# Expert stage of a hybrid layer: token rows by indirect DMA and transposes instead of a one-hot gather, second weights in whole rows into four banks, four more weight buffers

## The chip, the cores and the metric

One core of a Trainium2 chip runs the whole layer as one program. The metric is the device time of that program in microseconds: the median of several executions. The kernel before takes 2963.49 us, the median of 3 runs from 2961.25 to 2971.55.

## The reference, cut to what matters

512 tokens of width 2048 go through a layer: attention and RWKV-7 time mixing, an output projection, then a mixture of experts, then a final norm. Everything is float32. Each token goes to 2 of 32 experts (1024 choices in all), and an expert is a gated MLP of width 512:

```python
N_EXPERTS, TOP_K, D_MODEL, D_EXPERT = 32, 2, 2048, 512
h = rms_norm(x, norm_ffn_g) * (1 + sc2) + sh2
expert_idx, gates = hierarchical_route(h, w_grp, b_grp, w_exp, b_exp)
...
xb = x_pad[tok]                                    # rows of the expert's tokens
yb = (silu(xb @ w1[e]) * (xb @ w3[e])) @ w2[e]     # w1, w3: 2048 x 512, w2: 512 x 2048
y  = yb * gate[:, None]
out = zeros.at[slot_tok].add(y)                    # back to the tokens
...
x = x + g2 * out
return rms_norm(x, final_norm_g)
```

The weights of the 32 experts together are 402.65 MB, and all of them are read.

## The kernel before, in words

**Stages.** The program runs the input projection, the attention and the RWKV stage, then the output projection (`out_loop`, L1115), which leaves the residual stream in `xm`: 512 tokens as 4 groups of 128 partitions, 2048 columns each. `route_chunk` (L1267) takes each 512 columns of `xm` as they are finished, transposes them, multiplies them with the router's weights and sums squares for the norm. Then come the choice of experts (L1307 to L1414), the expert stage (L1416 to L1574), and the final norm (L1627 to L1640). A loop over tokens that overflow an expert's slots (L1585) stands behind the expert stage; it runs zero times here.

**Pairs.** Experts are worked in 16 pairs. Each expert has 64 slots, so a pair has 128 rows, and about half of them hold a token. Slot numbers and gates of the tokens are in `sg`; a row with no token is zero.

**Gather.** PE multiplies and adds one-hot matrices to select rows. For this `cut` (L1287) splits `xm` into three bf16 parts `xp0`, `xp1`, `xp2` whose sum is the float32 value; they take 48 KB of each partition. `onehots` (L1422) builds the one-hot matrix `ohb` of a pair on DVE, and by 12 matmuls (L1436) the row `rr` of the slots' norm factors, copied by ACT (L1439). `gather_units` (L1454) is a generator of 16 steps; together they are 192 bf16 matmuls of 128x128 (L1461), which give the tokens' columns already transposed. DVE multiplies with `rr` (L1465) and ACT applies the modulation (L1467) into `xT_`, 16 tiles of 128 columns.

**First layer.** For each quarter q of the 2048 columns, w1 (v = 0) and w3 (v = 1), each with four k and two experts e: a matmul of 64 columns by 512 (L1547), 64 in all. Expert e writes the partitions 64e to 64e + 63 of one PSUM bank, one bank for v = 0 and one for v = 1 (tag "h"). A matmul so uses half of PE's columns, and the two of a (k) use the two halves.

**Middle.** ACT takes the SiLU (L1555, once per pair: the pair's clock mark in the trace), DVE multiplies with the other bank and the gate (L1556), PE transposes (L1559), DVE copies to `gT` (L1561).

**Second layer.** For each 512 of the 2048 output columns n, four j and two experts: 32 matmuls (L1567) into a bank of tag "y" (2 banks). n is the outer loop.

**Scatter.** `scatter_units` (L1471) multiplies `py` with the residual gate (`yt`, L1475), splits it into two float32r parts (ACT cast L168, DVE difference L169), and for each of the 4 token groups multiplies with the one-hot matrix `ohT` (L1480, L1481) into the single bank of tag "o"; DVE adds it to `xm` (L1482). The four units of an n are put on the list `pend`, from which one is taken at each even k of the first layer and after each j of the second. `scatterers` (L1442) makes `ohT` and the gate column.

**Weights.** Each pair has 24 tiles of 1 MB, 16 of w1 and w3 and 8 of w2 (`srcs`). They go through a ring of seven buffers of 16 KB per partition (`fetch` L1210, `wtile` L1224): 2 in `Y` and 1 in `scr`, which are free by then, `NA` = 1 in one pool and `NB` = 3 in another. Nearly all are issued on SP's queue (L1221), each as soon as PE has done with the tile that had the buffer. A tile of w1 or w3 is read in rows of 8 KB; a tile of w2 takes 512 columns of 512 rows, 2 KB each.

**Order.** The program is recorded by the tile framework with a scheduler (`schedule_with_timeline_sim=True`): it simulates the engines and sets the order of each engine's list. The order in which the code emits steps is only its starting point, so gather, scatter and expert matmuls end up interleaved as the simulation had them ready. PE's order is fixed from then on.

PSUM in the expert stage: tags "g" 2 banks (gather), "t" 1, "o" 1, "h" 2, "y" 2.

Of the kernel before, what the change touches and what calls it, by code (L numbers as in the profile page):

```python
# [79 lines left out]
def layer(ctx, tc, tab, x, c, ctx_in, c_ctx, w_mod, b_mod, norm_attn_g, norm_ffn_g, w_in, shift_mu,  # L80
# [29 lines left out]
    r_r = dram.tile([NP0, 128, T], F32, name="r_r")  # L110

# [1080 lines left out]
    NY, NA, NB = 3, 1, 3  # L1192
# [4 lines left out]
    parts = [mq.tile([128, 4, 4, 4, 128], BF16, name=f"xp{i}") for i in range(3)]  # L1197
# [69 lines left out]
    def route_chunk(n):  # L1267
# [16 lines left out]
        if n < 3:  # L1284
            cut(n, ve)

    def cut(n, e):  # L1287
        for i in range(4):
            pa, pb, pc = (p_[:, i, n] for p_ in parts)
            v_ = xm[:, i, 512 * n:512 * n + 512].rearrange("t (p j) -> t j p", j=4)  # L1290
            res = t("res", [128, 4, 128])
            sc.copy(pa, v_)
            e.tensor_sub(res, v_, pa)
            sc.copy(pb, res)
            e.tensor_sub(pc, res, pb)
# [3 lines left out]
    for n in range(3, 4):  # L1299
        cut(n, gp)  # L1300
# [119 lines left out]
    new_psum("ps_moe", [("g", 2, 512), ("t", 1, 512), ("o", 1, 512), ("h", 2, 512), ("y", 2, 512)])  # L1420

    def onehots(pool, psum, base, n):  # L1422
# [10 lines left out]
        prr = psum()[:, 0:n]  # L1433
        for i in range(4):
            for k_ in range(3):
                te.matmul(prr, rb[:, k_, i:i + 1].to_broadcast([128, 128]), ohb[:, i], start=(i + k_ == 0),  # L1436
                          stop=(i + k_ == 5))
# [16 lines left out]
    def gather_units(pool, psum, ohb, rr, xT_, n):  # L1454
        for q in range(4):
            pg = psum()
            for j in range(4):
                first = True
                for part in parts:
                    for i in range(4):  # L1460
                        te.matmul(pg[:, j], part[:, i, q, j], ohb[:, i], start=first, stop=(part is parts[2] and i == 3))  # L1461
                        first = False
                if j == 3:
                    t_ = pool.tile([128, 4, n], F32, name="xr")
                    ve.tensor_mul(t_, pg, rr[:, None, :].to_broadcast([128, 4, n]))  # L1465
                    for jj in range(4):
                        sc.activation(xT_[:, 4 * q + jj], t_[:, jj], AF.Identity, bias=shc[:, q, jj:jj + 1],  # L1467
                                      scale=scc[:, q, jj:jj + 1])
                yield

    def scatter_units(pool, psum, py, ohT, n, np_, done=None):  # L1471
# [5 lines left out]

        def unit(i):
# [33 lines left out]
    for _ in range(4):  # L1512
        next(first)
# [152 lines left out]
```

## Time and profile before

| | before |
|---|---|
| median of 3 runs | 2963.49 us (2961.25 to 2971.55) |
| profiled execution, span | 2957.8 us |
| mean granted PE clock | 0.950 |
| PE busy | 2701.8 us, 91% |
| DVE, ACT, POOL busy | 1634.6, 734.9, 1056.0 us |
| moved by DMA | 715.28 MB, mean 242 GB/s |
| of it on the Pool queue | 75.11 MB |

The span is what the profiler saw from the first instruction to the last; the page gives no further time of that execution, so the span stands beside the median of the unprofiled runs, 5.7 us below it. A row of the profile names the line of the kernel, the engine, the operation and the tiles (out <- in), then counts and times. "PE" is the matmul itself, "PEld" the weight load that overlaps it. 128*64 in a matmul's row is the part of PE's array in use. The expert stage is the last 1.2 ms of the span, from the first SiLU at 1721.9 us on.

### The profile page before, as it was taken

The numbers are of one execution on the slowest core, as the hardware profiler recorded it, in microseconds if no ns is written. First come the engines' busy times: TensorE is split into PE (matmuls) and PEld (weight loads), VectorE is DVE, ScalarE is ACT, GpSimd is POOL, SyncE is SP. The second block draws the span as 40 slices with busy tenths as digits, with TensorE's granted clock in tenths as the row PEclk, the third lists the DMA queues.
The fourth block names the chain that finished last, engine by engine and source line by source line (L and its number), as shares of the span: only waits on it lengthen the run. The fifth ranks groups of instructions, "written<-read, shape, count | busy, mean of one in ns | idle before, by whom it ended". The sixth has DMA issues, their size and how long they took to land. (4 is left out here: it accounts for less than half of the span.)

```text
span 2957.8 us, 45065 instructions
## 1 busy us (share of the span) xinstructions
PE 2701.8 (91%) x18204; PEld 1671.2 (57%) x18204; DVE 1634.6 (55%) x2166; ACT 734.9 (25%) x1366; POOL 1056.0 (36%) x1077
## 2 busy tenths in 40 slices
PE   5999888999977999996888899999999999999995
PEld 3577777887856777884677644333333343333322
DVE  3365788776788777767978523332333332333334
ACT  4222332333333333332234221111111111111102
POOL 1078878067676777777675100000000000000000
PEclk9999898999978899998889899999999999999998
DMA  8955477666678578876563398888888888888996
GB/s 307 326 153 183 133 193 178 140 143 148 145 173 188 163 212 228 231 220 223 174 196 115 146 353 300 297 319 317 318 325 314 304 320 315 318 311 315 334 352 246
DMA packets 563683, 715.28 MB, mean 242 GB/s; under 512 B 319448, under 2 KB 398192, under 8 KB 529424
## 3 DMA queue, kind: packets, MB, share of 16 engines
q1 hardware_dynamic: 454480, 574.78, 59.4%
q0 software_dynamic: 21904, 75.11, 7.8%
q10 hardware_dynamic: 87088, 62.48, 7.2%
q8 instruction: 145, 2.38, 0.3%
q14 instruction: 66, 0.54, 0.1%
HBM read 642.91 MB, written 69.35 MB: 241 GB/s over the span
## 5 line engine op out<-in xcount | busy, mean ns | idle before, releaser
L1482 DVE TENSOR_TENSOR xm<-xm,pox 128x512 f32<-128x512 f32 x256 | 174.9, 687 | 531.3 <-PE pox L1481 531.3
L1636 POOL TENSOR_TENSOR xm<-xm,fgr 128x1024 f32<-128x1024 f32 x2 | 5.6, 2831 | 1271.2 <-ACT xm L1635 1271.2
L523 POOL TENSOR_TENSOR scr<-scr 128x512 f32<-128x512 f32 x240 | 344.7, 1436 | 8.6
L522 POOL TENSOR_TENSOR scr<-scr,scl 128x512 f32<-128x512 f32 x240 | 285.5, 1206 | 145.8 <-DMA scr<-in_w_mod_dram 145.4
L172 PE MATMUL acc<-hT,w 128*128 128x512 f32 (+1 forms) x752 | 269.4, 358 | 8.8 <-DVE km L275 7.4
L174 PE MATMUL acc<-hT,w 128*128 128x512 f32 (+1 forms) x752 | 268.6, 357 | 2.4 <-DVE w L169 2.4
L173 PE MATMUL acc<-hT,w 128*128 128x512 f32 (+1 forms) x752 | 268.4, 357 | 0.0
L1461 PEld LDWEIGHTS <-xp 128*128 128x128 bf16 x3072 | 173.9, 98 | 147.0 <-issue 146.6
L1461 PE MATMUL pg<-ohb,xp 128*128 128x128 bf16 x3072 | 214.3, 220 | 0.0
L1567 PE MATMUL py<-ew,gT 128*64 128x512 f32 x584 | 197.9, 610 | 6.3 <-DVE gT L1561 6.3
L169 DVE TENSOR_TENSOR w<-wraw,w 128x512 fp32r<-128x512 f32 (+1 forms) x132 | 123.3, 939 | 133.2 <-ACT w L168 132.2
L172 PEld LDWEIGHTS acc<-hT,w 128*128 128x128 f32 (+1 forms) x752 | 145.2, 193 | 31.4 <-ACT ks L271 7.5
L174 PEld LDWEIGHTS acc<-hT,w 128*128 128x128 f32 (+1 forms) x752 | 144.4, 192 | 24.6 <-DVE w L169 3.2
L173 PEld LDWEIGHTS acc<-hT,w 128*128 128x128 f32 (+1 forms) x752 | 144.9, 193 | 21.2 <-issue 1.5
L168 ACT CAST yr<-yt 128x512 fp32r<-128x512 f32 x64 | 39.5, 618 | 463.0 <-PE pox L1480 317.4
L518 POOL DMA_DIRECT2D scr<-in_w_mod_dram x128 | 94.5, 738 | 161.0 <-DVE scr L357 141.8
L168 ACT CAST w<-wraw 128x512 fp32r<-128x512 f32 (+1 forms) x132 | 81.0, 616 | 273.7 <-PE acc L173 148.5
L1480 PE MATMUL pox<-yr,ohT 128*128 128x512 f32 x256 | 123.7, 490 | 17.2 <-DVE xm L1482 13.0
L1480 PEld LDWEIGHTS pox<-yr,ohT 128*128 128x128 f32 x256 | 47.7, 187 | 150.7 <-issue 85.7
L1475 DVE TENSOR_TENSOR yt<-py,g2r 128x512 f32<-128x512 f32 x64 | 44.3, 692 | 140.2 <-PE py L1567 140.2
L1567 PE MATMUL py<-Y,gT 128*64 128x512 f32 x288 | 114.1, 616 | 3.1 <-DVE gT L1561 3.1
L478 POOL TENSOR_TENSOR scr<-scr 128x31 f32<-128x31 f32 (+15 forms) x155 | 106.5, 687 | 26.6 <-DMA scr<-r_ab 14.8
(696 smaller groups left out, 5824.1 us busy)
## 6 DMA issues: line engine op xcount, KB each, us to landing
ew<-in_w_dram SPq DMA_DIRECT2D x219, 1024.0 KB, 6.9
Y<-in_w_dram SPq DMA_DIRECT2D x110, 1024.0 KB, 6.8
scr<-in_w_mod_dram POOLq DMA_DIRECT2D x128, 512.0 KB, 5.1
scr<-in_w_dram SPq DMA_DIRECT2D x54, 1024.0 KB, 6.9
ld<-in_w_mod_dram SPq DMA_DIRECT2D x32, 1024.0 KB, 7.0
wraw<-in_w_in_dram ACTq DMA_DIRECT2D x104, 256.0 KB, 3.6
wor<-in_w_out_dram ACTq DMA_DIRECT2D x64, 256.0 KB, 3.5
QXr<-r_qx SPq DMA_DIRECT2D x24, 512.0 KB, 5.3
```

The lines of the kernel that those rows point to most:

```text
L168: sc.copy(hi, src)
L169: (lo_eng or ve).tensor_sub(lo, src, hi)
L172: te.matmul(out, lhs[0], rhs[0], start=first, stop=False)
L173: te.matmul(out, lhs[0], rhs[1], start=False, stop=False)
L174: te.matmul(out, lhs[1], rhs[0], start=False, stop=last)
L478: e.tensor_mul(z, xs.to_broadcast([128, n, m]), ms.to_broadcast([128, n, m]))
L522: gp.tensor_mul(wt[:, k], wt[:, k], s_)
L523: gp.tensor_add(macc, macc, wt[:, k])
L1461: te.matmul(pg[:, j], part[:, i, q, j], ohb[:, i], start=first, stop=(part is parts[2] and i == 3))
L1480: te.matmul(po, ohT[0:np_, 128 * i:128 * i + 128], yr[0], start=True, stop=False)
L1482: ve.tensor_add(xm[:, i, ns], xm[:, i, ns], po)
L1567: te.matmul(py[64 * e:64 * e + 64], gT[:, j, 64 * e:64 * e + 64], ws[e][:, j], start=(j == 0), stop=(j == 3))
```

## The change

- **Rows to DRAM.** `route_chunk` writes each 512 columns of `xm` to a DRAM tile `r_x` by SP's queue. `cut` and the three bf16 parts go.
- **Gather.** `fetch_rows` keeps the one-hot `ohb`, but multiplies it with `tokc`, 6 columns that hold the token number (low and high part) and the three bf16 parts of the norm factor: 4 matmuls of 6 columns. DVE sums them and makes an integer index; an indirect DMA from Pool fetches the rows into `xg` (two buffers, zeroed once), an index of 512 (no token) is out of bounds and fetches nothing; ACT scales the rows by the norm factor. `gather_units` has 4 steps: four float32 transposes into the "t" bank, and four ACT modulations. They are emitted in the first layer's loop at q = 2 and 3, after each v.
- **Second weights.** For pairs 0 to 14 a tile of w2 is 128 whole rows of 8 KB, so the loop over j is outside, n inside, with four open banks of "y". The last pair keeps the old layout and loop.
- **Scatters.** The units of a pair are put on `pend` at its end; `step` takes one at each odd k of the first layer and after each (j, n) of the second.
- **Buffers.** `NA` goes from 1 to 5: eleven weight buffers. PSUM: "t" 1, "o" 1, "h" 2, "y" 4.
- `scatterers` is called after the next pair's `prep`, and the overflow table (`oid`) is worked out behind the first pair's first layer. The overflow loop uses the new helpers.

```diff
+    r_x = dram.tile([T, D], F32, name="r_x")
...
-    NY, NA, NB = 3, 1, 3
+    NY, NA, NB = 3, 5, 3
...
-    parts = [mq.tile([128, 4, 4, 4, 128], BF16, name=f"xp{i}") for i in range(3)]
...
-            srcs += [w2v[2 * p_ + e, :, :, 512 * n:512 * n + 512] for e in range(2)]
+            if p_ < 15:
+                srcs += [w2[0, 2 * p_ + e, 128 * n:128 * n + 128, :] for e in range(2)]
+            else:
+                srcs += [w2v[2 * p_ + e, :, :, 512 * n:512 * n + 512] for e in range(2)]
...
+        sy.dma_start(r_x.rearrange("(i p) d -> p i d", p=128)[:, :, 512 * n:512 * n + 512],
+                     xm[:, :, 512 * n:512 * n + 512])
...
+    tokc = mk.tile([128, 4, 2, 3], BF16, name="tokc")
...
+        gp.tensor_copy(tokc[:, :, 1, k_], left[k_])
...
+    gp.tensor_copy(tokc[:, :, 0, 0], K["pcol"].to_broadcast([128, 4]))
+    gp.tensor_scalar(tokc[:, :, 0, 1], io[:, 0:4], 128.0, -512.0, op0=OP.mult, op1=OP.add)
...
-    new_psum("ps_moe", [("g", 2, 512), ("t", 1, 512), ("o", 1, 512), ("h", 2, 512), ("y", 2, 512)])
...
+    new_psum("ps_moe", [("t", 1, 512), ("o", 1, 512), ("h", 2, 512), ("y", 4, 512)])
+    xgs = [me.tile([128, D], F32, name=f"xg{i}") for i in range(2)]
+    for a_ in xgs:
+        gp.memset(a_, 0.0)
...
-        prr = psum()[:, 0:n]
+        pi = psum()[0:n, 0:6]
         for i in range(4):
-            for k_ in range(3):
-                te.matmul(prr, rb[:, k_, i:i + 1].to_broadcast([128, 128]), ohb[:, i], start=(i + k_ == 0),
-                          stop=(i + k_ == 5))
-        rr = pool.tile([128, n], F32, name="rr", bufs=2)
-        sc.copy(rr, prr)
-        return ohb, rr
+            te.matmul(pi, ohb[:, i], tokc[:, i].rearrange("p a b -> p (a b)"), start=(i == 0), stop=(i == 3))
+        ir = pool.tile([n, 2], F32, name="ir", bufs=2)
+        ve.tensor_reduce(ir, pi.rearrange("p (a b) -> p a b", a=2), axis=AX.X, op=OP.add)
+        ix = pool.tile([n, 1], I32, name="ix", bufs=2)
+        ve.tensor_scalar(ix, ir[:, 0:1], 512.0, None, op0=OP.add)
+        gp.indirect_dma_start(xg, None, r_x, bass.IndirectOffsetOnAxis(ap=ix, axis=0), bounds_check=T - 1,
+                              oob_is_err=False)
+        sc.mul(xg, xg, ir[:, 1:2])
...
-    def gather_units(pool, psum, ohb, rr, xT_, n):
+    def gather_units(psum, xg, xT_, n):
+        v_ = xg.rearrange("s (q p j) -> s q j p", p=128, j=4)
         for q in range(4):
-            pg = psum()
+            pg = psum(q)
             for j in range(4):
-                first = True
-                for part in parts:
-                    for i in range(4):
-                        te.matmul(pg[:, j], part[:, i, q, j], ohb[:, i], start=first, stop=(part is parts[2] and i == 3))
-                        first = False
-                if j == 3:
-                    t_ = pool.tile([128, 4, n], F32, name="xr")
-                    ve.tensor_mul(t_, pg, rr[:, None, :].to_broadcast([128, 4, n]))
-                    for jj in range(4):
-                        sc.activation(xT_[:, 4 * q + jj], t_[:, jj], AF.Identity, bias=shc[:, q, jj:jj + 1],
-                                      scale=scc[:, q, jj:jj + 1])
-                yield
+                te.transpose(pg[:, j], v_[:, q, j], ident[0:n, 0:n])
+            for j in range(4):
+                sc.activation(xT_[:, 4 * q + j], pg[:, j], AF.Identity, bias=shc[:, q, j:j + 1],
+                              scale=scc[:, q, j:j + 1])
+            yield
 
...
+    def step():
+        while pend:
+            if next(pend[0], 0) == 0:
+                pend.pop(0)
+            else:
+                break
...
+        psq = (lambda q: bank("ptg", [128, 4, 128], *(("t", 1), ("o", 1))[q % 2])) if p == 0 else \
+            (lambda q: bank("ptg", [128, 4, 128], "t", 1))
+        return [xT_, gather_units(psq, xg, xT_, 128)]
...
                     if k % 2:
-                        if p < 15:
-                            next(nxt[1], None)
-                    elif pend:
-                        pend.pop(0)()
+                        step()
+                if p < 15 and q > 1:
+                    next(cur_x[1], None)
...
+            pys = [bank("py", [128, 512], "y", 4) for _ in range(4)]
             for j in range(4):
-                for e in range(2):
-                    te.matmul(py[64 * e:64 * e + 64], gT[:, j, 64 * e:64 * e + 64], ws[e][:, j],
-                              start=(j == 0), stop=(j == 3))
-                if pend:
-                    pend.pop(0)()
-            last = p == 15
-            pend += scatter_units(me, psl if last else pso, py, ohT, n, 128, square if last else None)
-            while last and pend:
-                pend.pop(0)()
+                ws = [wtile(w0 + 16 + 2 * j + e) for e in range(2)]
+                for n in range(4):
+                    for e in range(2):
+                        te.matmul(pys[n][64 * e:64 * e + 64], gT[:, j, 64 * e:64 * e + 64], ws[e][:, n],
+                                  start=(j == 0), stop=(j == 3))
+                    step()
+            pend += [scatter_units(me, pso, pys[n], ohT, n, 128) for n in range(4)]
```

**What the scheduler made of it.** PE, second-layer phase of a steady pair before: L1567 alternates between the tiles of the two experts (`scr`, `Y`), all into one bank `py`.

```order
L1567 MATMUL py_17239<-scr_147,gT_17184 64x512
L1567 MATMUL py_17239<-Y_2235,gT_17184 64x512
L1567 MATMUL py_17239<-scr_147,gT_17184 64x512
L1567 MATMUL py_17239<-Y_2235,gT_17184 64x512
L1567 MATMUL py_17239<-scr_147,gT_17184 64x512
```

The same phase after (L1577): four banks, and past the first eight matmuls four of one expert (`ew_16816`), then four of the other (`ew_16818`).

```order
L1577 MATMUL py_16800<-ew_16816,gT_16798 64x512
L1577 MATMUL py_16801<-ew_16816,gT_16798 64x512
L1577 MATMUL py_16802<-ew_16816,gT_16798 64x512
L1577 MATMUL py_16803<-ew_16816,gT_16798 64x512
L1577 MATMUL py_16800<-ew_16818,gT_16798 64x512
L1577 MATMUL py_16801<-ew_16818,gT_16798 64x512
L1577 MATMUL py_16802<-ew_16818,gT_16798 64x512
L1577 MATMUL py_16803<-ew_16818,gT_16798 64x512
```

Before, the halves alternate in the runs of a steady pair; after, two or more of one half follow each other in most of the second layer. Before has one such place, in its first pair's first layer (L1547): `ew_14966` and `ew_14970` are tiles of the first expert, `ew_14968` and `Y` of the second.

```order
L1547 MATMUL ph_15247<-ew_14966,xT__15134 64x512
L1547 MATMUL ph_15247<-ew_14968,xT__15134 64x512
L1547 MATMUL ph_15248<-ew_14970,xT__15134 64x512
L1547 MATMUL ph_15247<-ew_14966,xT__15134 64x512
L1547 MATMUL ph_15247<-ew_14968,xT__15134 64x512
L1547 MATMUL ph_15248<-Y_2235,xT__15134 64x512
L1547 MATMUL ph_15248<-ew_14970,xT__15134 64x512
L1547 MATMUL ph_15248<-Y_2235,xT__15134 64x512
```

Numbering the halves 0 and 1, that is 0 1 0 0 1 1 0 1.

PE, first-layer phase of a steady pair after, where the scatters (L1472, L1473) and the transposes of the next pair's rows (L1458) stand:

```order
L1536 MATMUL ph_16881<-ew_16927,xT__16565 64x512
L1472 MATMUL pox_16961<-yr0_16936,ohT_16570 128x512
L1473 MATMUL pox_16961<-yr1_16937,ohT_16570 128x512
L1472 MATMUL pox_16969<-yr0_16936,ohT_16570 128x512
L1473 MATMUL pox_16969<-yr1_16937,ohT_16570 128x512
L1472 MATMUL pox_16987<-yr0_16982,ohT_16570 128x512
L1473 MATMUL pox_16987<-yr1_16983,ohT_16570 128x512
L1458 MATMUL ptg_16999<-k_ident_79,xg1_15044 128x128 x4
L1536 MATMUL ph_16881<-ew_16929,xT__16565 64x512
```

Three scatter units now follow each other, with no expert matmul between them.

ACT, one pair before, from its SiLU (L1555) on: the gather's modulation (L1467) and the casts of the scatter (L168) alternate.

```order
L1555 ACTIVATE scr_147<-ph_17339 128x512
L1439 COPY rr_17816<-prr_17803 128x128
L1467 ACTIVATE xT__17818<-xr_17917,cols_13942 128x128 x4
L168 CAST yr0_17688<-yt_17687 128x512
L1467 ACTIVATE xT__17818<-xr_17994,cols_13942 128x128 x4
L168 CAST yr0_17722<-yt_17721 128x512
L1467 ACTIVATE xT__17818<-xr_18072,cols_13942 128x128 x4
L168 CAST yr0_17757<-yt_17756 128x512
L1467 ACTIVATE xT__17818<-xr_18148,cols_13942 128x128 x4
L168 CAST yr0_17791<-yt_17790 128x512
```

ACT, one pair after, from its SiLU (L1552): the row scaling (L1439) stands ahead of the last cast (now L169), and all four modulations (L1460) behind it.

```order
L1552 ACTIVATE scr_148<-ph_16268 128x512
L169 CAST yr0_16585<-yt_16584 128x512
L169 CAST yr0_16629<-yt_16628 128x512
L169 CAST yr0_16675<-yt_16674 128x512
L1439 ACTIVATE xg0_15043<-xg0_15043,ir_16557 128x2048
L169 CAST yr0_16737<-yt_16736 128x512
L1460 ACTIVATE xT__16565<-ptg_16692,cols_13940 128x128 x4
L1460 ACTIVATE xT__16565<-ptg_16721,cols_13940 128x128 x4
L1460 ACTIVATE xT__16565<-ptg_16754,cols_13940 128x128 x4
L1460 ACTIVATE xT__16565<-ptg_16782,cols_13940 128x128 x4
```

The casts moved ahead of the modulations, and the wait for the fetched rows stands among them.

More of the change, by code (lines that the diff above doesn't have):

```diff
@@ L1476, in scatter_units @@
         split(yr[0], yr[1], yt)
-        def unit(i):
+        for i in range(4):
             po = psum()
@@ L1484, in unit @@
                 done(i, n)
-        return [lambda i=i: unit(i) for i in range(4)]
+            yield
     pbank = lambda name, shape, tag, bufs: (lambda: bank(name, shape, tag, bufs))
-    psg = pbank("pg", [128, 4, 128], "g", 2)
     pst = pbank("prr", [128, 512], "t", 1)
@@ L1539, in layer @@
         for q in range(4):
-            for _ in range(4 if p == 0 and q else 0):
-                next(first)
             for v in range(2):
@@ L1558, in layer @@
         for j in range(4):
-            te.transpose(pt[:, j, :], g_[:, j::4], ident)
+            te.transpose(pt[:, j, :], g_[:, j::4] if last else g_[:, 128 * j:128 * j + 128], ident)
         gT = me.tile([128, 4, 128], F32, name="gT")
         ve.tensor_copy(gT, pt)
-        for n in range(4):
-            py = bank("py", [128, 512], "y", 2)
-            ws = [wtile(w0 + 16 + 2 * n + e) for e in range(2)]
-            for j in range(4):
-                for e in range(2):
-                    te.matmul(py[64 * e:64 * e + 64], gT[:, j, 64 * e:64 * e + 64], ws[e][:, j],
-                              start=(j == 0), stop=(j == 3))
-                if pend:
-                    pend.pop(0)()
-            last = p == 15
-            pend += scatter_units(me, psl if last else pso, py, ohT, n, 128, square if last else None)
-            while last and pend:
-                pend.pop(0)()
+        if last:
+            for n in range(4):
+                py = bank("py", [128, 512], "y", 4)
+                ws = [wtile(w0 + 16 + 2 * n + e) for e in range(2)]
+                for j in range(4):
+                    for e in range(2):
+                        te.matmul(py[64 * e:64 * e + 64], gT[:, j, 64 * e:64 * e + 64], ws[e][:, j],
+                                  start=(j == 0), stop=(j == 3))
+                    step()
+                pend.append(scatter_units(me, psl, py, ohT, n, 128, square))
+                while pend:
+                    step()
+        else:
+            pys = [bank("py", [128, 512], "y", 4) for _ in range(4)]
+            for j in range(4):
+                ws = [wtile(w0 + 16 + 2 * j + e) for e in range(2)]
+                for n in range(4):
+                    for e in range(2):
+                        te.matmul(pys[n][64 * e:64 * e + 64], gT[:, j, 64 * e:64 * e + 64], ws[e][:, n],
+                                  start=(j == 0), stop=(j == 3))
+                    step()
+            pend += [scatter_units(me, pso, pys[n], ohT, n, 128) for n in range(4)]
     mes.close()
@@ L1589, in layer @@
                 opb = lambda name, shape, bufs=1: (lambda: op_.tile(shape, F32, name=name, bufs=bufs))
[L1590 removed]
+                oxg = ol.tile([64, D], F32, name="oxg")
+                gp.memset(oxg, 0.0)
+                fetch_rows(ol, opb("opi", [128, 512]), cur, 64, oxg)
                 ohT, ga = scatterers(ol, cur)
                 xT_ = ol.tile([128, KT, 64], F32, name="oxT")
[L1593 removed]
+                for _ in gather_units(lambda q: op_.tile([128, 4, 64], F32, name="opg"), oxg, xT_, 64):
                     pass
@@ L1619, in layer @@
                         te.matmul(py, gT[:, j, :], wt[:, j], start=(j == 0), stop=(j == 3))
-                    for u in scatter_units(ol, opb("opo", [128, 512]), py, ohT, n, 64):
-                        u()
+                    for _ in scatter_units(ol, opb("opo", [128, 512]), py, ohT, n, 64):
+                        pass
                 ve.tensor_scalar(cur, cur, 64.0, None, op0=OP.add)
```

62 lines of the change are left out of this document (23 added, 39 removed).

## The prediction

> **What bounds the kernel now.** I read the stages first, then the waits, then single pairs of experts. The windows from the first SiLU on (PE, PEld, DVE, ACT and POOL busy, PE clock, DMA share, GB/s):
>
> ```profile
> core 0: us, PE busy (x) PEld busy (x) DVE busy (x) ACT busy (x) POOL busy (x), PEclk, DMA share, GB/s
> 1722.00:1796.00 74.00, 74.00 (x471) 31.54 (x468) 21.77 (x35) 11.38 (x26) 0.00 (x0) 1.00 0.90 339
> 1796.00:2758.00 962.00, 933.49 (x5236) 378.67 (x5237) 312.89 (x469) 116.40 (x265) 0.00 (x0) 0.99 0.86 315
> 2831.00:2898.00 67.00, 61.77 (x234) 19.86 (x232) 17.82 (x26) 3.49 (x6) 0.00 (x0) 1.00 0.96 370
> ```
>
> PE is busy 97% of the long window while the DMA engines are at 0.86. Who waits for whom between 1800 and 2800 us, PE first, then the SP queue:
>
> ```profile
> PE pth L1559 <- DVE scr L1556: 11.9, 12, 1.8
> PE pox L1480 <- DVE xm L1482: 9.7, 13, 0.8
> PE py L1567 <- DVE gT L1561: 9.4, 12, 0.8
> SPq L1221 <- PE ph L1547: 504.5, 169, 7.3
> ```
>
> No row has PE waiting for weights; weights wait for PE to free a buffer. So PE's own list is the bound, and a pair of experts takes the time from one SiLU to the next:
>
> ```profile
> L1555 ACT ACTIVATE scr<-ph x16: 597/597/600, 1721.9 to 2897.6; 128x512 f32<-128x512 f32 x16
> 1796.06 0.60 ACT L1555 ACTIVATE scr<-ph 128x512 f32<-128x512 f32 x1 [15.70 <-PE ph L1547]
> 2757.93 0.60 ACT L1555 ACTIVATE scr<-ph 128x512 f32<-128x512 f32 x1 [30.57 <-PE ph L1547]
> 2831.34 0.60 ACT L1555 ACTIVATE scr<-ph 128x512 f32<-128x512 f32 x1 [30.16 <-PE ph L1547]
> ```
>
> The 12 periods from 1796.06 to 2757.93 average 80.2 us; the first is 74.2, the last two 73.4 and 66.2.
>
> **The change part by part: PE's list for one pair.** Prices come from start-to-start times on PE (a float32 matmul leaves two records, so x12 is six matmuls):
>
> ```profile
> 2006.67 2.80 PE L1547 MATMUL ph<-Y,xT__16840 128*64 128x512 f32 x12
> 2009.39 0.84 PE L1461 MATMUL pg<-ohb,xp 128*128 128x128 bf16 x12
> 2010.17 1.07 PE L1547 MATMUL ph<-scr,xT__16840 128*64 128x512 f32 x2
> 2011.17 0.50 PE L1480 MATMUL pox<-yr,ohT 128*128 128x512 f32 x1
> 2109.66 0.40 PE L1481 MATMUL pox<-yr,ohT 128*128 128x512 f32 x1
> 2110.83 0.50 PE L1480 MATMUL pox<-yr,ohT 128*128 128x512 f32 x1 [0.78 <-DVE xm L1482]
> 2111.17 0.39 PE L1481 MATMUL pox<-yr,ohT 128*128 128x512 f32 x1
> 2111.49 1.08 PE L1547 MATMUL ph<-ew,xT__17329 128*64 128x512 f32 x4
> ```
>
> Six expert matmuls take 2.72, one alone 1.00. Two of them, one for each expert's 64 columns, share a step of 0.86, an odd one has a step alone, and a run pays 0.14 for the switch. A scatter (L1480, L1481) takes 0.66; one behind another on the single "o" bank adds 1.17 - 0.33 = 0.84, since DVE must empty the bank.
>
> *Expert matmuls.* Both kernels have 96 to a pair. In the order of before, a steady pair cuts them into 23 runs, 20 odd: 58 steps x 0.86 + 23 x 0.14 = 53.1 us. After: 14 runs, 12 odd, 54 steps, 48.4. **-4.7.**
>
> *Gather, row scale, index.* 192 bf16 matmuls and 12 for the scale go; four of 6 columns come. Long runs give the price:
>
> ```profile
> 1682.97 6.37 PE L1461 MATMUL pg<-ohb,xp 128*128 128x128 bf16 x111
> 1689.27 1.08 PE L1547 MATMUL ph<-ew,xT__15134 128*64 128x512 f32 x4
> 2047.22 1.46 PE L1436 MATMUL prr<-ohb,rb 128*128 128x128 bf16 x12
> 2048.62 1.12 PE L1567 MATMUL py<-Y,gT 128*64 128x512 f32 x2
> ```
>
> 6.30/111 = 0.057 each: **-10.9**. The scale's 1.40 falls to four matmuls, between 4/12 of it and all: I take 0.5, **-0.9.**
>
> *Transposes.* Sixteen of float32 per pair, in four groups; the router's are the same shape:
>
> ```profile
> 1644.30 0.75 PE L1273 MATMUL pt<-k_ident,xm 128*128 128x128 f32 x4 [1.05 <-DVE xm L1132]
> 1644.90 0.30 PE L1277 MATMUL plg<-wrs,xmT 128*128 128x36 f32 x1
> 1688.12 1.65 ACT L1467 ACTIVATE xT__15134<-xr,cols 128x128 f32<-128x128 f32 x4 [0.81 <-DVE xr L1465]
> ```
>
> 4 x 0.60 = **+2.4**. All use the one "t" bank, and ACT needs 1.65 to empty it. In the order the closest two groups have one expert matmul and a scatter between them (1.00 + 0.66), so PE waits about **+0.3**.
>
> *Scatters move.* All 16 now stand in the next pair's first-layer phase, and stand bunched: four back-to-back places per pair instead of one: 3 x 0.84 = **+2.5**. The first must wait for yt, cast and difference, which the last matmuls on the later banks cover.
>
> *Second layer in four banks.* The built order no longer alternates the halves: after eight matmuls that do, it gives four of one expert, then four of the other. If PE started matmuls strictly in order, 24 of them would need 19 steps, 16.2 us; perfectly shared, 12 and 10.3. Before has one run like that in small, in its first pair, halves 0 1 0 0 1 1 0 1:
>
> ```profile
> 1693.33 2.36 PE L1547 MATMUL ph<-ew,xT__15134 128*64 128x512 f32 x9
> 1696.97 0.34 PE L1461 MATMUL pg<-ohb,xp 128*128 128x128 bf16 x3
> ```
>
> The eight took 3.64 us. Four shared steps are 3.44 + 0.14 = 3.58; strict order needs a fifth, 4.44. So one matmul waiting for its half does not hold back the other half. With one such place per half the 24 need 14 steps (the second half starts two late) where the run starts with four alike, 12 where it goes on from the eight; about half the pairs are of each kind: **+0.9**, bounds 0 and 6. [...]
>
> Sum: -4.7 - 10.9 - 0.9 + 2.4 + 0.3 + 2.5 + 0.9 = -10.4, so a steady pair takes 69.8 us.
>
> *Weights.* A pair now also fetches its token rows, on average 64 of 8 KB (1024 choices over 16 pairs): 25.17 + 0.52 = 25.7 MB in 69.8 us is 368 GB/s. What the engines gave when kept full, on 8 KB rows, then mostly on the second layer's 2 KB rows:
>
> ```profile
> 1738.00:1758.00 20.00, 20.00 (x109) 7.42 (x105) 5.94 (x9) 4.08 (x10) 0.00 (x0) 1.00 1.02 420
> 2826.00:2850.00 24.00, 20.85 (x86) 6.77 (x82) 7.96 (x11) 1.83 (x3) 0.00 (x0) 1.00 1.02 364
> ```
>
> With all rows at 8 KB the cover is 420 against 368, 61 us of transfer under 70 of PE. The second-layer phase now eats 8 tiles in some 14 us, 600 GB/s; eleven buffers instead of seven hold that. At 364 the pair would be 70.6.
>
> *The fetch itself.* Index, Pool issue, landing, scaling on ACT, then the transposes:
>
> ```profile
> scr<-in_w_mod_dram POOLq DMA_DIRECT2D x128, 512.0 KB, 5.1
> L518 POOL DMA_DIRECT2D scr<-in_w_mod_dram x128 | 94.5, 738 | 161.0 <-DVE scr L357 141.8 <-POOL scr L523 14.0 <-DMA r_tt<-scr 3.2
> 2941.03 2.19 ACT L1635 ACTIVATE xm<-xm,rms_r 128x1024 f32<-128x1024 f32 x2 [1.83 <-DVE rms_r L232]
> ```
>
> The order puts the index matmuls some 25 to 30 us of PE work ahead of the first transposes. DVE 1, Pool 0.7 and scaling 2.2 (two halves of 1.1) leave 21 to 26 us for landing; half a megabyte from the Pool queue landed in 5.1. Cost **0**; each microsecond past the cover costs PE one, and ACT's cast for the last scatters stands behind the scaling.
>
> *Ends.* The stage: 12 x 10.4 = 125; the first period, 74.2, becomes about 67.5 (7); the last two, 139.6 together, become 69.8 + 65.5 (4): **-136**. Ahead of it go the 16 splits of tokens into three bf16 parts, and the router's small loads move up the SP queue, past the token loads:
>
> ```profile
> PEld pcl L1252 <- issue: 7.2, 1, 7.2
> PEld po_r L173 <- DVE wo L169: 10.8, 8, 2.8
> 1675.90 1.94 PE L1547 MATMUL ph<-Y,xT__15134 128*64 128x512 f32 x8
> ```
>
> PE's wait of 7.2 for a modulation row, and part of its waits for DVE, can go; I take 5, bounds 0 and 18. The first pair loses its interleaved gather (16.8 us on PE between 1680 and 1722) but puts fetch, scaling and a transpose group ahead of the first matmul now at 1675.90 (3 to 8 us more than the matrix gather), and the second pair's transposes, ordered behind the first SiLU, cost about 10: I take -3, bounds +6 and -8. Four 1 MB writes of tokens to DRAM go to an SP queue that is idle there. Together **-8.** The tail is unchanged.
>
> In all -144. The profiled span is 2957.8; the runs' median, 2963.5, lies 5.7 above it, which I keep: 2813.8 + 5.7 = 2819.5, say **2820 us**.
>
> **The rivals.**
> *Strict order on PE.* Every second-layer run of 24 to 28 costs 16.2 instead of about 11.1: 5.1 x 13 pairs = +67, **2887**. For it: only two alike in a row were seen to pass. Against: they did, three times in the first pair.
> *Transfers become the bound.* If a pair gets no more than the 339 GB/s of the first window, 25.7 MB take 75.8 us: 6.0 x 15 = +90, **2910**. For it: gather and weights share engines. Against: 420 at 1.02 share. [...]
> *Late rows: slower.* The gather is built row by row by Pool and shares the engines with up to nine queued tiles. If one lands after 40 us instead of about 8, PE stands 16 us in every pair at the first transposes: +240, **3060**. It decides from a landing of 24 + 144/15 = 34 us on. Against: 5.1.
> *More goes than I count.* The router's waits go wholly and the runs share fully: -12 - 12, **2795** or less.
>
> **How the numbers follow.** Forecast (2795 to 2850) 0.66, strict order 0.13, transfers 0.08, late rows 0.05 (0.03 of it slower than before, the rest around 2870 to 2950), more than counted 0.08. The range 2795 to 2890 holds the forecast and strict order, 0.79. A measurement here can tell about 0.3% from no change, 9 us; faster by more 0.95, within 0.02, slower 0.03.
>
> **What would show it.** SiLU to SiLU 69 to 71 us; no L1461; PE waits at pox x4 per pair of 0.8; a run of 24 second-layer matmuls in 10.3 to 12 us (16 says strict order); no PE wait on weights (if there, transfers), none at the transposes for xg (if there, late rows); DMA share about 0.9 at 370 GB/s. A pair above 73 us, or a first SiLU later than 1722, makes the sum wrong.

## The result: 2848.65 us, and the profile after

The changed kernel takes 2848.65 us (median of 4 runs, 2836.86 to 2861.77), the kernel before on the same chip 2962.37 us (2946.09 to 2971.55). The ratio is 0.9628, 95% interval 0.9593 to 0.9664: 3.7% faster, 114 us between the medians. The forecast was 2820 us, the range 2795 to 2890. The profiled execution has a span of 2846.8 us, 111.0 less than before, where 144 were forecast. So the direction and the larger part are right, and 33 us are missing. The time lies 1 us inside the band of the forecast (2795 to 2850). The number alone does not tell whether PE's list or the transfers set it; the experiments do.

The SiLU of each pair, and the stages from the first SiLU on (PE, PEld, DVE, ACT, POOL busy, PE clock, DMA share, GB/s), of the changed kernel:

```profile
L1552 ACT ACTIVATE scr<-ph x16: 597/597/598, 1711.7 to 2786.0; 128x512 f32<-128x512 f32 x16
```

```profile
1711.70:1784.00 72.30, 63.18 (x247) 22.35 (x244) 16.73 (x28) 15.90 (x32) 1.09 (x1) 0.93 1.01 420
1784.00:2649.40 865.40, 798.88 (x2996) 287.80 (x2998) 285.16 (x445) 134.47 (x273) 14.60 (x12) 0.98 0.90 358
2649.40:2786.00 136.60, 127.52 (x478) 44.15 (x476) 39.77 (x59) 14.04 (x27) 1.00 (x1) 0.99 0.94 372
```

The boundaries are SiLUs, so the rows answer to the forecast's steps. First SiLU 1711.7 (forecast 1713.9), first period 72.3 (67.5). These two belong together: the forecast booked about 10 us for the second pair's transposes ahead of the first SiLU, and they lie behind it. The second SiLU comes at 1784.0 (1781.4). The 12 middle periods 865.4 / 12 = 72.1 each (69.8): they carry 28 of the 33 missing us. The last two 136.6 together (135.3). The 15 periods average (2786.0 - 1711.7) / 15 = 71.6 us; before it was (2897.6 - 1721.9) / 15 = 78.4. This mean over 15 is the yardstick for all kernels below. The granted clock fell: 1.00, 0.99, 1.00 before in the three stages, now 0.93, 0.98, 0.99. In the first period that is one place, right behind the first SiLU, where PE waits four times 1.6 us for ACT among the second pair's transposes (bank "t") and those of the SiLU:

```profile
1719.00:1730.00 11.00, 6.30 (x20) 3.08 (x22) 0.69 (x1) 3.68 (x10) 0.00 (x0) 0.55 1.02 422
```

PE's waits in the changed kernel between 1800 and 2650 us, in the columns of the rows shown before (total, times, longest):

```profile
PE pox L1472 <- DVE xm L1474: 45.4, 54, 1.8
PE pth L1556 <- DVE scr L1553: 10.1, 11, 0.9
PE py L1577 <- DVE gT L1558: 8.6, 11, 0.8
```

The wait for the scatter's bank was 9.7 us in 13 places between 1800 and 2800; it is now 45.4 in 54. No row has PE waiting for weights, nor, in these pairs, for fetched rows.

The second layer of two pairs on PE (start, length, then the row; two records are one matmul):

```profile
2015.52 0.25 PE L1432 MATMUL prr<-tokc,ohb 128*128 128x6 bf16 x4
2015.71 12.51 PE L1577 MATMUL py<-ew,gT 128*64 128x512 f32 x48
2028.15 0.50 PE L1472 MATMUL pox<-yr,ohT 128*128 128x512 f32 x1
...
2155.69 3.65 PE L1577 MATMUL py<-ew,gT 128*64 128x512 f32 x8 [0.78 <-DVE gT L1558]
2159.27 0.25 PE L1432 MATMUL prr<-tokc,ohb 128*128 128x6 bf16 x4
2159.46 7.68 PE L1577 MATMUL py<-ew,gT 128*64 128x512 f32 x29
...
2173.68 0.51 PE L1472 MATMUL pox<-yr,ohT 128*128 128x512 f32 x1
```

The run of 24 takes 2028.15 - 2015.71 = 12.44 us. The first eight of that second layer, which alternate, take another 3.6 ahead of the index matmuls (L1432), from 2011.93 on. In the other pair the index matmuls stand behind the first four: those take 3.58, four steps and a switch, as matmuls of one half that share with nothing do; the 28 behind them take 14.22. So a second layer costs 16.0 or 17.8 us, where the forecast had 14.8 on average.

A chain of scatters in the first layer, and the windows around it:

```profile
2044.26 0.50 PE L1472 MATMUL pox<-yr,ohT 128*128 128x512 f32 x1
2044.60 0.40 PE L1473 MATMUL pox<-yr,ohT 128*128 128x512 f32 x1
2045.77 0.50 PE L1472 MATMUL pox<-yr,ohT 128*128 128x512 f32 x1 [0.78 <-DVE xm L1474]
2046.11 0.40 PE L1473 MATMUL pox<-yr,ohT 128*128 128x512 f32 x1
2047.38 0.49 PE L1472 MATMUL pox<-yr,ohT 128*128 128x512 f32 x1 [0.87 <-DVE xm L1474]
2047.69 0.61 PE L1473 MATMUL pox<-yr,ohT 128*128 128x512 f32 x1
2048.09 1.05 PE L1458 MATMUL ptg<-k_ident,xg 128*128 128x128 f32 x4
2049.08 4.63 PE L1536 MATMUL ph<-ew,xT__16258 128*64 128x512 f32 x14
```

```profile
2044.00:2047.40 3.40, 1.75 (x6) 0.64 (x5) 1.43 (x3) 0.62 (x1) 0.00 (x0) 1.00 1.02 393
2047.40:2050.80 3.40, 3.40 (x10) 1.64 (x12) 1.29 (x2) 1.50 (x4) 0.00 (x0) 0.54 0.48 200
2050.80:2054.20 3.40, 3.40 (x14) 1.29 (x11) 0.00 (x0) 0.00 (x0) 0.00 (x0) 0.96 0.19 24
```

PE is busy for 1.75 of 3.4 us while three scatters follow each other, and for the next 3.4 us the granted clock is 0.54. The seven matmuls that begin in it take 4.56 us instead of 3.58. This is a cost that the forecast doesn't have at all.

This is no single case. The trace's record of the granted clock has 10 falls to one half between 1740 and 2700 us, each 3.4 us long, against 5 in before between 1740 and 2850. Cut on the raster of 3.413 us on which the falls lie, the stretch ahead of a fall had PE busy for 0.39 to 0.54 of it in the changed kernel and 0.36 to 0.50 in before. No stretch in which PE was busy for 0.55 or more was followed by a fall; one at 0.49 (after) and one at 0.52 (before) were not followed by one either.

### The profile page after: what moved, and what is told of

The parts are those of the page before. It is cut to its first block, busy times and chain, and to the rows that moved or that the text cites. A ratio compares the mean times of both kernels' runs of the same rounds, so it can differ in the third digit from the quotient of the medians.

```text
span 2846.8 us, 39057 instructions
## 1 busy us (share of the span) xinstructions
PE 2525.3 (89%) x15260; PEld 1546.0 (54%) x15260; DVE 1554.9 (55%) x2110; ACT 730.8 (26%) x1334; POOL 1062.7 (37%) x1089
## 5 line engine op out<-in xcount | busy, mean ns | idle before, releaser
L1437 POOL DMA_INDIRECT xg<-r_x,ix x16 | 19.5, 1216 | 973.0 <-DVE sp L1422 711.2
L1577 PE MATMUL py<-ew,gT 128*64 128x512 f32 x680 | 197.4, 620 | 9.4 <-DVE gT L1558 9.4
L169 ACT CAST yr<-yt 128x512 fp32r<-128x512 f32 x64 | 39.6, 619 | 562.6 <-DVE yt L1468 354.5
L1472 PE MATMUL pox<-yr,ohT 128*128 128x512 f32 x256 | 125.6, 496 | 57.7 <-DVE xm L1474 53.6
L1472 PEld LDWEIGHTS pox<-yr,ohT 128*128 128x128 f32 x256 | 47.6, 187 | 224.7 <-DVE xm L1474 119.2
L169 ACT CAST w<-wraw 128x512 fp32r<-128x512 f32 (+1 forms) x132 | 81.0, 616 | 270.5 <-PE acc L174 148.8
L1577 PEld LDWEIGHTS py<-ew,gT 128*64 128x64 f32 x680 | 65.2, 141 | 111.1 <-issue 97.6
L479 POOL TENSOR_TENSOR scr<-scr 128x31 f32<-128x31 f32 (+15 forms) x155 | 106.7, 688 | 27.4 <-DMA scr<-r_ab 15.6
L480 POOL TENSOR_TENSOR scr<-scr 128x31 f32<-128x31 f32 (+15 forms) x155 | 109.6, 707 | 12.2
L1473 PE MATMUL pox<-yr,ohT 128*128 128x512 f32 x256 | 102.0, 406 | 0.3
```

Of the source, the lines that this page charges most:

```text
L169: sc.copy(hi, src)
L479: e.tensor_mul(z, xs.to_broadcast([128, n, m]), ms.to_broadcast([128, n, m]))
L480: e.tensor_add(xo, xo, z)
L1472: te.matmul(po, ohT[0:np_, 128 * i:128 * i + 128], yr[0], start=True, stop=False)
L1577: te.matmul(pys[n][64 * e:64 * e + 64], gT[:, j, 64 * e:64 * e + 64], ws[e][:, n], start=(j == 0), stop=(j == 3))
```

## The experiments

The theory, called A below: a pair takes what PE's list takes, with three prices: a matmul that waits for its half of the array holds back only the next of its own half (12.44 us for the run of 24, where strict order would be 16.2); a scatter behind a scatter costs 0.84 us, with waits for DVE of 0.78 and 0.87 in the rows above; a stretch of about 3.4 us with PE half busy (1.75 us) is paid for with a stretch at half clock (0.54). The main rival, B: the pair of 71.5 us is 25.7 MB at 359 GB/s, and the transfers set it. The long window shows 358 GB/s at a DMA share of 0.90, and this alone does not exclude the rival; that takes a kernel that moves more. (The pairs of 71.5 in the expectations are the 11 from the third SiLU on.)

### seven: seven weight buffers

```diff
-    NY, NA, NB = 3, 5, 3
+    NY, NA, NB = 3, 1, 3
```

> The changed kernel with seven weight buffers (NA = 1) instead of eleven; nothing else. Theory A, PE's list: a pair is bound by what PE does in order; seven buffers still hold the second layer's burst (8 tiles in 17 us; 5 are there, 3 more come at 2.5 us each), so pairs stay at 71 to 72 us and the time at about 2847, within 10. Rival, the four buffers carry the change: PE waits for weights in the second layer, 8 MB at 420 GB/s take 20 us instead of 16.8, 3 us more a pair, about 2893, with rows of L1577 waiting for DMA.

Measured: 2852.06 us, ratio to before 0.9644 (0.9586 to 0.9702); the changed kernel had 0.9628.

```profile
L1552 ACT ACTIVATE scr<-ph x16: 597/597/598, 1708.3 to 2791.2; 128x512 f32<-128x512 f32 x16
```

72.2 us a pair instead of 71.6, and no row of PE waiting for weights. A buffer holds one tile of 1 MB, which is 8 KB of each partition, not 16. In this kernel the four more buffers are worth nothing that can be measured: the two ratios differ by 0.2%, well inside their intervals.

### nobytes: the fetch moves no rows

```diff
-        ve.tensor_scalar(ix, ir[:, 0:1], 512.0, None, op0=OP.add)
+        ve.tensor_scalar(ix, ir[:, 0:1], 2048.0 if base in [128.0 * i for i in range(2, 16)] else 512.0, None, op0=OP.add)
```

> The changed kernel with the index of pairs 2 to 15 set out of bounds, so that the fetch is issued, waited for and scaled as before but moves no rows (these pairs then work on rows of earlier pairs). Theory A: the fetch is hidden, pairs stay at 71.5 and the time at 2848, within 10. Rival B, transfers: 0.52 of 25.7 MB less at 359 GB/s is 1.4 us a pair, 20 us, about 2828. Rival late rows: what PE loses to the landing comes back, at least 1 us a pair.

Measured: 2845.87 us, ratio 0.9607 (0.9553 to 0.9661).

```profile
L1552 ACT ACTIVATE scr<-ph x16: 597/597/599, 1713.7 to 2788.1; 128x512 f32<-128x512 f32 x16
```

71.6 us a pair with the rows and without them. The fetched bytes are hidden, B's 1.4 us a pair did not come, and nor did the late rows' price.

### old2, old2seven: the second layer as before

```diff
-            if p_ < 15:
+            if p_ < 0:
...
-        last = p == 15
+        last, fin_ = True, p == 15
...
-                pend.append(scatter_units(me, psl, py, ohT, n, 128, square))
-                while pend:
+                pend.append(scatter_units(me, psl if fin_ else pso, py, ohT, n, 128, square if fin_ else None))
+                while fin_ and pend:
```

> The changed kernel with the second layer as before: 2 KB rows of w2, n outer, j inner, for all pairs (eleven buffers and the row fetch stay). Theory A, PE's list: the halves alternate again and some scatters move back into the second layer; the order priced with before's steps is 2.2 us a pair shorter than the changed kernel's, so pairs of about 69.3 and 2818. Rival B, transfers: the pair of 71.5 is 25.7 MB at 359 GB/s and the engines set it; 2 KB rows are slower still (364 against 420 GB/s when full), so 3 us a pair more, about 2890.

> Only the gather's exchange: the changed kernel with the second layer as before and seven buffers. Theory A: row fetch and transposes carry nearly the whole gain; pairs of 69 to 70, about 2820. Rival, buffers and whole rows carry it: 2890 or more, since before's 80.2 less 11.8 for the gather, plus 3 for waits on weights, is 71.4 and the scatters' stalls stay.

Measured: old2 2832.6 us, ratio 0.9552 (0.9495 to 0.9609); old2seven (old2 with the edit of seven) 2832.17 us, 0.9572 (0.9537 to 0.9607).

```profile
L1552 ACT ACTIVATE scr<-ph x16: 597/597/598, 1718.0 to 2779.9; 128x512 f32<-128x512 f32 x16
```

```profile
L1552 ACT ACTIVATE scr<-ph x16: 597/597/598, 1720.5 to 2784.9; 128x512 f32<-128x512 f32 x16
```

70.8 and 71.0 us a pair. The exchange of the gather carries the whole gain, together with what old2seven keeps of the rest (`step`, which hands out the scatter units, and the place of `scatterers`); those were not tried apart. Whole rows of w2 in four banks did not add to it; by the medians they took 16 us away (2848.65 against 2832.6), though the intervals of the two ratios overlap. The expectation of 2818 was 15 too low. B's 2890 is excluded.

### joint2, joint: tiles of both experts

A w2 tile of joint2 holds half a row of each of the two experts, so whenever a tile is there, PE has work for both halves and the scheduler's list alternates.

```diff
-                srcs += [w2[0, 2 * p_ + e, 128 * n:128 * n + 128, :] for e in range(2)]
+                srcs += [w2[0, 2 * p_:2 * p_ + 2, 128 * n:128 * n + 128, 1024 * h:1024 * h + 1024].rearrange("e p d -> p e d")
+                         for h in range(2)]
...
-                        te.matmul(pys[n][64 * e:64 * e + 64], gT[:, j, 64 * e:64 * e + 64], ws[e][:, n],
+                        te.matmul(pys[n][64 * e:64 * e + 64], gT[:, j, 64 * e:64 * e + 64], ws[n // 2][:, 2 * e + n % 2],
```

joint does the same with w1 and w3:

```diff
-                srcs += [wv[2 * p_ + e, q] for e in range(2)]
+                srcs += [wv[2 * p_:2 * p_ + 2, q, :, 1024 * h:1024 * h + 1024].rearrange("e p d -> p e d") for h in range(2)]
...
-                        te.matmul(ph[v][64 * e:64 * e + 64], xT_[:, kt, 64 * e:64 * e + 64], ws[e][:, k],
+                        te.matmul(ph[v][64 * e:64 * e + 64], xT_[:, kt, 64 * e:64 * e + 64], ws[k // 2][:, 2 * e + k % 2],
```

> The changed kernel with each w2 tile of pairs 0 to 14 made of both experts (half a row of each, 4 KB packets) instead of whole rows of one. PE's list then alternates the halves through the whole second layer. Theory A: the second layer falls from 16 to 17.8 us to about 14.0, pairs from 71.5 to 68.4, the time to about 2805. Rival B, transfers: 25.7 MB a pair are still to come at 359 GB/s, pairs stay at 71.5 and the time at 2848. By the rival of strict order on PE, too, alternation gives 14.0.

> The changed kernel with every weight tile of pairs 0 to 14 (w1, w3 and w2; for pair 15 w1 and w3) made of both experts, 4 KB packets: when a tile is there, PE has work for both halves. In PE's list 8 runs of expert matmuls in all are odd, against 186 in the changed kernel. Theory A, PE's list: the order's price falls by 8.8 us a pair, pairs from 71.5 to about 62.5, unless 25.7 MB at 420 GB/s (61.2 us) stand in the way; about 2725. Rival B, transfers at 359 GB/s: pairs stay at 71.5, 2848. Between the two: the engines give 390 GB/s, pairs of 66, 2770.

Measured: joint2 2803.3 us, ratio 0.9457 (0.9401 to 0.9512); joint 2719.24 us (2712.73 to 2730.01), 0.9209 (0.9171 to 0.9247).

A second layer of joint2 on PE; its 24 alternating matmuls take 10.52 us instead of 12.51:

```profile
2003.49 10.52 PE L1582 MATMUL py<-ew,gT 128*64 128x512 f32 x48
```

The pairs of joint2, then those of joint, and two windows from the middle of joint's stage:

```profile
L1557 ACT ACTIVATE scr<-ph x16: 597/597/597, 1713.1 to 2744.5; 128x512 f32<-128x512 f32 x16
```

```profile
L1557 ACT ACTIVATE scr<-ph x16: 597/597/600, 1702.6 to 2647.4; 128x512 f32<-128x512 f32 x16
```

```profile
1836.00:2205.00 369.00, 344.28 (x1482) 120.47 (x1478) 139.95 (x220) 66.02 (x132) 7.59 (x6) 1.00 1.03 409
2205.00:2590.00 385.00, 359.15 (x1497) 124.03 (x1498) 138.82 (x214) 66.03 (x132) 6.70 (x6) 0.97 1.03 407
```

68.8 and 63.0 us a pair, both within 6 us of what A gave for the whole (2805 and 2725). B falls: the same bytes come at 407 to 409 GB/s, so 358 was PE's pace, not a limit. joint is the best kernel of the study, 129 us below the changed kernel by the medians. Its edit alters only which bytes share a tile, but the scheduler's list changes with it, and not only in the order of the halves. PE's waits in joint between 1860 and 2600 us:

```profile
PE pox L1477 <- DVE xm L1479: 18.7, 24, 0.8
PE py L1582 <- DMA ew<-in_w_dram: 2.7, 3, 1.4
```

With 7.0 more for ACT's cast, the waits at the scatters are 2.2 us a pair; in the changed kernel 45.4 us in 11.8 pairs were 3.8. PE's busy time on ph and py falls from 52.9 to 45.8 us a pair (from the third SiLU to the 14th). So of the 8.6 us that a pair gains some 7 lie in the sharing of the halves and 1.6 in the scatters. At a DMA share of 1.03 the engines always have work, yet PE's waits for weights come to 3.7 us in the 740, 0.3 a pair. The transfers have caught up with PE's list in joint; that they set its pace is not shown.

### two_o: a second bank for the scatters, shared with the transposes

```diff
-    pso = pbank("pox", [128, 512], "o", 1)
+    no = [0]
+
+    def pso():
+        no[0] += 1
+        return bank("pox", [128, 512], "ot"[no[0] % 2], 1)
```

> The changed kernel with the scatter matmuls alternating between the banks o and t instead of o alone. Theory A: the four places a pair where PE waits 0.8 us for DVE to empty the bank go (3.4 us), and with them the half-clock stretches that follow three such waits in a row (about 1 us in half of the pairs); pairs of 67.5, about 2795. Rival B, transfers: pairs stay at 71.5, 2848. A third: the transposes also need bank t and ACT takes 1.5 us to empty it, so the stalls move there and little is won, 2835.

Measured: 2867.87 us, ratio 0.9707 (0.9671 to 0.9743): slower than the changed kernel, where 2795 was expected. The end of a pair on PE, and a window from there:

```profile
2074.27 0.50 PE L1472 MATMUL pox<-yr,ohT 128*128 128x512 f32 x1 [1.60 <-ACT xT__16565 L1460]
2074.61 0.46 PE L1473 MATMUL pox<-yr,ohT 128*128 128x512 f32 x1
2075.85 1.13 PE L1458 MATMUL ptg<-k_ident,xg 128*128 128x128 f32 x4 [0.78 <-DVE xm L1474]
2078.57 1.12 PE L1560 MATMUL pth<-k_ident,scr 128*128 128x128 f32 x4 [1.60 <-ACT xT__16565 L1460]
2080.47 14.91 PE L1581 MATMUL py<-ew,gT 128*64 128x512 f32 x53 [0.78 <-DVE pc L1443]
```

```profile
2074.00:2082.00 8.00, 4.57 (x14) 2.28 (x16) 5.24 (x7) 1.72 (x5) 0.00 (x0) 0.55 0.64 270
```

The third case of the expectation came, and worse: the scheduler put the last transposes, a scatter and the SiLU's transposes next to each other at the end of the pair, all on bank t, and each waits 1.60 for ACT or 0.8 for DVE. PE is busy 4.57 of 8 us and the clock falls to 0.55, into the second layer. The waits did not go, they moved to a place where they are longer.

### joint_two: both edits

joint's diff and two_o's together.

> Both edits: tiles of both experts for all weights, and scatters in two banks. Theory A: the list's price falls to 59 to 61 us a pair, below the 61.2 that 25.7 MB take at 420 GB/s: the transfers become the bound, pairs of 62 to 64, about 2720, and PE's waits turn into waits for weights. Rival B, transfers at 359 GB/s: 2848.

Measured: 2724.39 us, ratio 0.9207 (0.9172 to 0.9241), the same as joint. Its middle:

```profile
1860.00:2600.00 740.00, 684.73 (x2948) 245.62 (x2950) 272.50 (x433) 131.69 (x264) 14.29 (x12) 0.99 1.03 409
```

Again 409 GB/s at 1.03. In that window PE's waits for DVE at the scatters are 14.2 us (18.7 in joint), but its waits for weights 13.2 (3.7 in joint): what the second bank saves comes back as waits for weights, as expected. Here the transfers begin to bind.

### old2_o3: three banks for the scatters, none shared

On top of old2's edit. With n outermost two banks of y are enough, and the two that are free go to o.

```diff
-    new_psum("ps_moe", [("t", 1, 512), ("o", 1, 512), ("h", 2, 512), ("y", 4, 512)])
+    new_psum("ps_moe", [("t", 1, 512), ("o", 3, 512), ("h", 2, 512), ("y", 2, 512)])
...
-    pso = pbank("pox", [128, 512], "o", 1)
+    pso = pbank("pox", [128, 512], "o", 3)
```

> The kernel of old2 (second layer as before: 2 KB rows, n outer) with two banks for y and three for the scatters' o; the transposes keep bank t for themselves. Theory A, stalls and clock: PE no longer waits for DVE between scatters and no half-clock stretch follows; the list's price falls from 67.2 to 63.3 us a pair, old2's measured pair of 70.6 to 65 to 67 (the scatters now stand closer behind yt and its cast, which may take 1 to 2 us back), about 2765 to 2790. Rival, half clock comes from something else (a lower mean load, transfers): the low stretches stay, pairs above 69, 2815 or more.

Measured: 2735.88 us, ratio 0.9274 (0.9243 to 0.9306), 29 us better than the near end of the expectation. PE's largest wait between 1860 and 2600 us, and that window, of old2:

```profile
PE pox L1472 <- DVE xm L1474: 33.8, 41, 0.9
```

```profile
1860.00:2600.00 740.00, 675.21 (x2604) 236.04 (x2602) 245.57 (x384) 112.34 (x224) 12.71 (x11) 0.97 0.94 367
```

and of old2_o3, with its SiLU row:

```profile
PE pox L1472 <- ACT yr L169: 11.9, 8, 1.5
```

```profile
1860.00:2600.00 740.00, 702.93 (x2822) 255.82 (x2823) 259.32 (x411) 127.94 (x256) 12.60 (x11) 0.99 1.01 397
```

```profile
L1552 ACT ACTIVATE scr<-ph x16: 597/597/598, 1703.3 to 2671.8; 128x512 f32<-128x512 f32 x16
```

The wait for the bank is gone and the clock is back at 0.99. The list was expected to save 3.9 us a pair; 64.6 us a pair are 6.2 below old2's 70.8. The rest is more than the waits: from the third SiLU to the 14th PE's busy time on pox falls from 12.1 to 9.7 us a pair, and on ph and py from 50.9 to 49.6. Why the scatter matmuls themselves get shorter, and how much of this is half clock that went, was not separated. This also moves 397 GB/s with the 2 KB rows of w2: rows of 2 KB for a third of the bytes do not hold the engines at 364.

### joint_seven: joint with seven buffers

> The kernel of joint with seven weight buffers instead of eleven; the list's price is the same, 60.7 us a pair. Joint moves 409 GB/s at a DMA share of 1.03, so the transfers bound it as much as PE does. Theory: now the buffers matter, because a queue that stands still while PE is in a slow place loses time that it can't win back: 1 to 3 us a pair, 2735 to 2765, with rows of PE waiting for the weights' DMA. Rival: seven buffers hold here too, 2719 within 10.

Measured: 2729.89 us, ratio 0.9259 (0.9226 to 0.9292); joint has 0.9209 (0.9171 to 0.9247). 0.5% by the centres, with intervals that just touch: 11 us, less than the theory's 16 to 46 and at the edge of the rival's 10. If the buffers matter where the transfers bind, it is by no more than this; it stays open.

### joint1_o3: old2_o3 with joint tiles for w1 and w3

> The kernel of old2_o3 with w1 and w3 tiles made of both experts, as in joint (w2 keeps 2 KB rows). PE's list falls from 63.3 to 61.2 us a pair. Theory A: pairs fall by the same 2 us from 64.8 to 62.7 and the time to about 2706, unless the transfers bind first. Rival: they do; 25.7 MB at the 397 GB/s of old2_o3, whose DMA share is 1.01 already, are 64.7 us, and the time stays at 2736.

Measured: 2739.57 us, ratio 0.9241 (0.9183 to 0.9299), no better than old2_o3. The same window, and PE's largest wait for weights, of which old2_o3's list of waits shows none:

```profile
1860.00:2600.00 740.00, 694.40 (x2896) 252.70 (x2898) 268.09 (x422) 130.90 (x262) 13.01 (x11) 1.00 1.03 401
```

```profile
PE ph L1540 <- DMA ew<-in_w_dram: 6.9, 12, 0.7
```

The rival was right for the time, and only in part for the pairs: they take 64.0 us instead of 64.6, where A had 2 less. PE's waits for weights are 10.3 us in the window, 0.9 a pair, and its waits for ACT's cast rose from 11.9 to 17.8. Besides, the first SiLU of this run comes at 1714.1, 10.8 later than in old2_o3, and this hides the 9 us that the stage gained. Why it comes later was not looked into.

## Why the prediction was right, and where 33 us went

- **Gather, row scale, index, transposes.** Right. L1461 is gone. The four index matmuls take 0.19 us (2015.52 to 2015.71) instead of the 0.5 taken, and PE has no wait at the transposes in the steady pairs, where 0.3 was taken. old2seven shows that this exchange, with how the scatter units are handed out, makes the kernel 4.3% faster than before.
- **Fetch hidden.** Right in the steady pairs: DVE's sum and index take 0.17 and 0.15 us (1 taken for both), ACT's scaling 2.0 (2.2 taken), Pool's issue 1.0 to 1.4 (0.7 taken); rows land 6.0 to 10.2 us after the issue, and nobytes is no faster. In the first pair nothing hides the fetch, and PE waits for the scaled rows 10.6 us. That is not yet the cost: from the first index matmuls to the first expert matmul it is 12.8 us against 8.0 with the matrix gather, 4.8 more, within the 3 to 8 taken.

```profile
PE ptg L1458 <- ACT xg L1439: 10.6, 1, 10.6
```

- **Ahead of the stage, -8.** The mechanism was partly wrong, and luck covers it. The wait for a modulation row, which was to bring most of 5 us, stands in the changed kernel as it did before:

```profile
PEld pcl L1255 <- issue: 7.2, 1, 7.2
```

  The first index matmuls start 3.3 us later than before (1671.24 against 1667.95). The first layer of the first pair is 18.3 us shorter (27.7 against 46.0), 16.8 taken. Without the 10 us that lie behind it, the first SiLU was due at about 1704; it looks 2 us early only because these 10 were booked ahead of it.
- **Expert matmuls, -4.7, and second layer, +0.9.** The step that failed is the second: the term was mis-sized. A second layer takes 16.0 or 17.8 us, and the forecast had 14.8 on average; so the term is nearer +3 than +0.9. PE's busy time on ph and py (8 periods of before, 11 of after), half-clock stretches included, is

```profile
1961.00:2599.70 638.70, 284.98 (x1026) 76.41 (x1024) 6.01 (x8) 4.79 (x8) 0.99 0.86 316
1961.00:2599.70 638.70, 155.65 (x512) 39.36 (x512) 22.13 (x32) 0.99 0.86 316
```

```profile
1862.80:2649.40 786.60, 395.39 (x1410) 108.22 (x1408) 8.26 (x11) 6.58 (x12) 0.98 0.91 361
1862.80:2649.40 786.60, 186.61 (x704) 65.36 (x704) 30.41 (x44) 0.98 0.91 361
```

  Per pair that is 35.6 + 19.5 = 55.1 before and 35.9 + 17.0 = 52.9 after: -2.2 instead of -3.8. The run of 24 was forecast right for the pairs that start with four alike (14 steps and a switch, 12.2; measured 12.44, where strict order would be 16.2, or 16.3 by 19 steps of 0.86). The other kind was forecast at 12 steps, "where it goes on from the eight". There the index matmuls cut the run after its first four, which then share with nothing: 17.8 us instead of 13.9. They stand in the order of the changed kernel; the prediction counted their price and not what they cut.
- **Strict order on PE.** Excluded, by 12.44 against 16.2, and by joint2, which gains 1.99 us on 24 matmuls and not 5.7.
- **Scatters bunched, +2.5.** Right in kind and nearly in size: 9.7 us of bank waits in 1000 us (12.5 pairs of 80.2) became 45.4 in 850 (11.8 of 72.1), 0.78 and 3.85 a pair, so +3.1. There are 4.6 such waits a pair, four were forecast.
- **The clock.** Not in the sum. By the stage rows PE lost 0.07 x 72 + 0.02 x 865 + 0.01 x 137 = 24 us of clock, before 0.01 x 962 = 10. So up to 14 us of the 33. The falls themselves say the same: 9 in the 12 middle periods of the changed kernel, with PE busy throughout, lose 9 x 1.7 = 15 us, 5 in before's 12 lose 8.5. That half clock follows PE standing half idle is what these falls and the rows of two_o show; in old2_o3, with the waits gone, the clock is back at 0.99 from old2's 0.97. No run changed the clock alone.
- **Weights.** The cover was right (no wait of PE for weights between 1800 and 2650 us), and joint shows that 407 to 409 GB/s can be kept up over 750 us.
- **Median against span.** The 5.7 kept between them was 1.9 here; so of the 33 us missing in the span 29 are left between 2820 and the median of 2848.65.

A middle period lacks 2.3 us. As an estimate from these rows, the second layer gives +2.1 (16.9 against 14.8), the bank waits +0.6, the clock +0.6 and the index matmuls -0.3: 3.0, more than is missing. The terms overlap, since some half-clock stretches lie in second layers, and no run separates them. Of the prediction's own signs two were missed narrowly: 72.1 us from SiLU to SiLU (69 to 71) and 12.44 us for a run of 24 (10.3 to 12).

## What to carry to other kernels

Where two column halves of PE work for two experts, lay a weight tile out so that it feeds both: a list that a scheduler fills tile by tile then alternates by itself, and the kernel built so was 129 us faster here, more than the change under study gave, some 7 of 8.6 us a pair by the sharing and the rest by fewer waits at the scatters. Short waits in a row cost twice here, once as waits (0.78 and 0.87 us) and once as clock (0.54 for the next 3.4 us): count how often they leave PE half idle for 3.4 us, and give the result that is drained a bank of its own, not one that another step also waits for. And a rate that holds over a long window does not prove that the transfers set the pace: 358 GB/s over 865 us became 407 to 409 in joint, where PE asked for more.

## What was not expected of the hardware

- A window of 3.4 us in which PE was busy 1.75 was followed by 3.4 us at a granted clock of 0.54. All 15 falls counted from 1740 us on (to 2850 in before, to 2700 in after) followed a stretch of 3.4 us in which PE was busy for 0.36 to 0.54 of it; no single wait there was longer than 1.8 us.
- Column-half matmuls are timed as if they overtook one waiting matmul of the other half: 0000 1111 repeated took 12.44 us for 24, between full sharing (10.5 in joint2) and the 16.2 worked out for strict order.
- With 2 KB rows for a third of the bytes the engines moved 397 GB/s over 740 us, 364 being what a 24 us window of before had shown.
